# Layer 0's weight remainders: from subtractions on GpSimd to an accumulating DMA that GpSimd issues

## The chip, the cores and the metric

The kernel runs on one core of a Trainium2 chip. The metric is the device time of one execution in microseconds (us), lower is better; a kernel's time is the median of its runs. The engines are called as in the profile: PE is TensorE (PEld its weight loads), DVE is VectorE, ACT is ScalarE, POOL is GpSimd, SP is SyncE.

## The reference

One inference step of a two-layer trunk on 640 tokens of width 1024: a prompt of 128 and a latent grid of 512 (8 rows of 64). Layer 0 is a Conformer convolution branch, layer 1 a bidirectional Mamba-2 branch. The change lies in layer 0's first projection:

```python
def conformer_branch(h, on_grid, w_in, b_in, w_dw, b_dw, ln_g, ln_b, w_out):
    u = h @ w_in + b_in                       # 1024 -> 6144
    a, a_gate, z = jnp.split(u, 3, axis=-1)   # 2048 each
    v = a * jax.nn.sigmoid(a_gate)
    ...
    v = depthwise_conv(v, w_dw, b_dw).reshape(nb, length, e)   # 31 taps
    v = jax.nn.silu(layer_norm(v, ln_g, ln_b))
    return (v * jax.nn.silu(z)) @ w_out
```

All of it is float32. Before a layer come RMSNorm and a shift and scale computed from the condition (adaLN); after it comes a gated residual add.

## The kernel before

**Products in three parts.** TensorE multiplies `float32r` operands. To keep float32's precision each operand is split into a high part (a cast to `float32r`) and a low part (the value less its high part). A product is three matmuls into the same PSUM tile: high weight by high activation, high by low, low by high. A weight tile is 128 partitions x 1024 columns (512 KB); one holds all of `w_in` for 128 output columns. It is loaded by SP into `wf`, cast by ACT into `wh`, and the difference of `wf` and `wh` is written to `wl`. `wf` has two buffers, `wh` and `wl` three each. One output tile of layer 0 takes 48 matmuls: 8 chunks of the width, 2 halves of 320 tokens, 3 parts.

**Layer 0's stage.** The 6144 columns are 48 tiles: `a0` to `a15`, `g0` to `g15` (gates), `z0` to `z15`. Three are multiplied as the activations appear (`g0`, `a0`, `g1`). The other 29 `a` and `g` tiles and `z0` to `z6` stand in a list (`PLAN0`, line 457) and are multiplied in that order; the rest of `z` is multiplied behind it, under the layer norm (`z_more`, `in_tile`, `split_w`). A finished `g` tile goes through ACT's sigmoid (`after_g`, line 511, tile `sg`); the `a` tile is multiplied with it on DVE (`after_a`, line 527, tile `v`). `z` tiles go through ACT's silu (`after_z`, line 543). These steps free the PSUM buffers of the products, of which there are two (`mm`). Beside some `g` tiles PE multiplies blocks of adaLN weights (line 582), whose sums ACT copies out as `ada_row` (line 516) and PE turns (line 122).

**The convolution of `v`** is shared out by tap. ACT starts the sum in PSUM (line 625, `cva`); DVE adds most taps to it (line 633). The outer taps (`NPOOL`, 4 to 11 of 30 for each tile) are scaled by ACT into `tp` (line 664; three buffers) and added by POOL to `cv` (line 705), into which ACT first copies `cva` (line 640). POOL also makes the corrections where the two halves of the tokens meet (`seam`, lines 689 to 699). For tiles 14 and 15 POOL sums separately and DVE adds its sum at the end (line 653). `cv` and its square then feed the layer norm's column sums (line 190), at the end `pst`; then follow the statistics (lines 783 to 799) and the normalisation (lines 805 to 811).

**What sets the order.** Between `run = Order(PRIO0)` and `run.run()` the order of all five queues is planned at build time. Each chain of steps is a Python generator that yields steps (engine, planned duration), waits for keys (`key`), and takes and returns buffers (`get`, `put`). The planner keeps a clock for each engine, always emits the step that can start first (ties by `PRIO0`), and the emitted order is each engine's order: an engine never overtakes in its own queue. A step may name two engines (`either`); the later one must win by its bias. The chain `weights` loads the weight tiles, and starts for each a chain `split` (from line 474). There the cast is planned with 1.05 us on ACT; the subtraction with 2.41 on POOL or 1.23 on DVE, at a bias of 9.0 against DVE for all but the first tile. At its end `wf` is returned and the key `("w", m)` posted, on which `product(m)` waits; `product` returns `wh` and `wl` after its last matmul. The planner's clocks shape the order only; on the chip the engines wait on semaphores.

```python
for name, n in (("wf", 2), ("wh", 1), ("wl", 1), ("mm", 0), ("tm", 2), ("v", 4), ("cva", 2), ("cs", 32), ("tp", 3), ("pr", 1), ("eb", 3)):
    run.ring(name, n, 1.0 if name == "cs" else -9.0)
```

Of the kernel before, what the change touches and what calls it, by code (L numbers as in the profile page):

```python
# [7 lines left out]
F32 = mybir.dt.float32  # L8
F32R = mybir.dt.float32r
I32 = mybir.dt.int32  # L10
AF = mybir.ActivationFunctionType
ALU = mybir.AluOpType
# [29 lines left out]
def trunk(ctx: ExitStack, tc: tile.TileContext, a: dict):  # L42
# [5 lines left out]
    V, S, G, T = nc.vector, nc.scalar, nc.gpsimd, nc.tensor  # L48
# [186 lines left out]
    PE, ACT, VE, PO, SP, VL = range(6)  # L235

    class Order:
# [14 lines left out]
        def post(self, key, t):  # L252
            assert key not in self.keys, key
            self.keys[key] = t

        def put(self, name, t):
            self.rings[name].append(t)
# [73 lines left out]
    def op(eng, dur, fn, table=None):  # L331
        return "op", ((eng, dur, fn, table),)

    def either(*ways, bias=2.0):
        return "op", tuple((e_, d_, f_, None) for e_, d_, f_ in ways), bias
# [4 lines left out]
    def get(name):  # L340
        return "get", name
# [62 lines left out]
    with tc.tile_pool(name="l0", bufs=1) as lp:  # L404
# [29 lines left out]
        for i in range(3):  # L434
            t = lp.tile([P, 2, 30], F32, name=f"eb{i}")
# [24 lines left out]
        post, put, start = run.post, run.put, run.start  # L460
# [3 lines left out]
        tiles0 = [{"a": 0, "g": 16, "z": 32}[n[0]] + int(n[1:]) for n in plan if n[0] != "s"]  # L464
        W0 = {}

        def weights():
            for m in tiles0 + order[:2]:
                yield get("wf")
                wf = gp.tile([P, 1024], F32, tag="wf", bufs=2, name="wf")  # L470
                t = yield op(SP, 0.35, lambda: nc.sync.dma_start(out=wf, in_=a["w_in1"][m]))
                start(split(m, wf), t)

        def split(m, wf):
            yield get("wh")
            wh = gp.tile([P, 1024], F32R, tag="wh", bufs=3, name="wh")
            yield op(ACT, 1.05, lambda: S.copy(out=wh, in_=wf))  # L477
            yield get("wl")
            wl = gp.tile([P, 1024], F32R, tag="wl", bufs=3, name="wl")
            t = yield either((PO, 2.41, lambda: G.tensor_sub(out=wl, in0=wf, in1=wh.bitcast(F32))), (VL, 1.23, lambda: V.tensor_sub(out=wl, in0=wf, in1=wh.bitcast(F32))), bias=0.0 if m == tiles0[0] else 9.0)  # L480
            put("wf", t)
            W0[m] = wh, wl
            post(("w", m), t)
            if m in order[:2]:
                ahead.append((m, W0[m]))
# [271 lines left out]
        def w_next():  # L757
            w_out1(2)
            return wahead.pop(0)
# [77 lines left out]
        for pi, (m0, nm) in enumerate(((0, 2), (2, 4), (6, 2))):  # L837
# [3 lines left out]
            for kp in range(8):  # L841
                wh, wl = w_next()
# [4 lines left out]
            for j in range(nm):  # L847
                m = m0 + j
# [49 lines left out]
    if True:  # L898
# [8 lines left out]
        for i in range(2):  # L907
            t = lp.tile([P, 646], F32, name=f"up{i}")
# [19 lines left out]
        def tr(name):  # L928
            return lp.tile([P, NT], F32, tag="yhl", bufs=8, name=name)[:, 0:384]
# [4 lines left out]
        xr, rp, e, q, t, u, v, one = (tr(n) for n in ("xr", "rp", "e", "q", "t", "u", "v", "one"))  # L934
# [7 lines left out]
        post, put, start = run.post, run.put, run.start  # L942
# [14 lines left out]
        def w_load(i, src):  # L957
            cell = {}

            def load():  # L960
                cell["wf"] = gp.tile([P, 1024], F32, tag="wf", bufs=2, name="wf")
                nc.sync.dma_start(out=cell["wf"], in_=src)

            def high():
                cell["wh"] = gp.tile([P, 1024], F32R, tag="wh", bufs=3, name="wh")
                S.copy(out=cell["wh"], in_=cell["wf"])  # L966

            def low(e_):
                cell["wl"] = gp.tile([P, 1024], F32R, tag="wl", bufs=3, name="wl")
                e_.tensor_sub(out=cell["wl"], in0=cell["wf"], in1=cell["wh"].bitcast(F32))  # L970

            def split():
                yield get("wh")
                yield op(ACT, 1.05, high)
                yield get("wl")
                t = yield either((VL, 1.22, lambda: low(V)), (PO, 2.41, lambda: low(G)), bias=PRIO["low"])
                put("wf", t)
                W[i] = cell["wh"], cell["wl"]
                post(("w", i), t)

            yield get("wf")
            t = yield op(SP, 0.35, load)
            start(split(), t)
# [859 lines left out]
```

## Time and profile before

| | us |
|---|---|
| runs, median (3 runs) | 1106.04 (1104.78 to 1108.8) |
| the profiled execution, its own time | 1107.31 |
| its span, first to last instruction | 1105.5 |

The mean clock granted to PE was 0.986 of full speed. The kernel read 109.80 MB from HBM and wrote 4.92 MB.

How to read it: the page's first part gives busy time, share of the span and number of instructions for each engine; its second part cuts the span into 40 equal slices (27.6 us each) with the busy share in tenths. A row of a stage gives busy time and count of each engine in it, then the granted clock, the share of time that the 16 DMA engines were busy, and GB/s. A row of waits reads: who waited, line, for whom; total us, times, longest. A group's row gives the line, engine, operation, output and inputs with shapes, the count, then busy time and the mean in ns, then idle time before it and what ended that. A row of the timeline gives start and length in us, the engine, the instruction, and in brackets the idle time before it and what ended it. DMA issues aren't counted as busy time. An engine that is idle off the path that sets the end costs nothing. Matmuls overlap, so the length of one (0.31 us) is twice the 0.147 us between two.

### The profile page before, as it was taken

What the parts mean: (1) busy time and instruction counts of PE and PEld (TensorE: products, weight loads), DVE (VectorE), ACT (ScalarE), POOL (GpSimd) and SP (SyncE); (2) the same over time, 40 slices, a digit from 0 to 9 for tenths busy, and PEclk for the clock granted to TensorE, in tenths of its full rate; (3) what the DMA queues carried; (4) which work ended last, traced back from release to release, by engine and by line L of the source; (5) the groups of instructions that cost most, each with busy time, mean ns of one, the idle gap of its engine ahead of it and who ended that gap; (6) DMA issues with size and microseconds to landing.
All of it is one profiled execution on the core that took longest, in us unless ns stands there. A gap on an engine that the chain in (4) does not pass through costs nothing.

```text
span 1105.5 us, 19815 instructions
## 1 busy us (share of the span) xinstructions
PE 1057.0 (96%) x7896; PEld 980.5 (89%) x7896; DVE 816.4 (74%) x1156; ACT 590.5 (53%) x1021; POOL 521.1 (47%) x447
## 2 busy tenths in 40 slices
PE   6999899999988999999999999999999999999996
PEld 4899899998987999999999887899889888978896
DVE  2589989999889379513369789988765786767673
ACT  6546566656665466312267657493546473653442
POOL 1059999978999637300000065414551443244213
PEclk9999999999989999999999999999999999999997
DMA  9364244332212111523302363424342424343102
GB/s 360 155 210 134 70 142 133 117 133 66 69 58 77 57 40 37 193 68 116 124 10 100 96 155 105 109 73 125 101 106 90 115 64 109 109 121 95 39 20 95
DMA packets 79052, 116.00 MB, mean 105 GB/s; under 512 B 26096, under 2 KB 49008, under 8 KB 78960
## 3 DMA queue, kind: packets, MB, share of 16 engines
q1 hardware_dynamic: 78240, 113.92, 33.6%
q8 instruction: 62, 1.02, 0.4%
q10 hardware_dynamic: 720, 0.82, 0.2%
q14 instruction: 30, 0.25, 0.1%
HBM read 109.80 MB, written 4.92 MB: 104 GB/s over the span
## 4 chain that ended last, share of the span: by engine, by line
PE 56%; DVE 21%; POOL 9%; ACT 6%; issue 4%; DMA 3%; SPq 1%; POOLq 0%; DVEq 0%; ACTq 0%
DVE cva L633 9%; PE pz L1004 8%; PE o L1004 8%; PE xs L1004 6%; POOL cv L705 5%; PE o L1513 3%; PE po L1285 2%; PE pst L1222 2%; PE B L1004 2%; DVE cn L805 2%; DVE xs L1046 2%; PE py L1353 2%; POOL wl L480 2%; DVE wl L970 1%; PE C L1004 1%
## 5 line engine op out<-in xcount | busy, mean ns | idle before, releaser
L633 DVE SCALAR_TENSOR_TENSOR cva<-v,cst,cva 128x620 f32<-128x620 f32 (+11 forms) x359 | 276.0, 820 | 15.3 <-ACT cva L625 11.1
L705 POOL TENSOR_TENSOR cv<-cv,tp 128x490 f32<-128x490 f32 (+5 forms) x121 | 144.6, 1195 | 8.1
L664 ACT ACTIVATE tp<-v,cst 128x490 f32<-128x490 f32 (+5 forms) x121 | 85.7, 722 | 83.3 <-POOL cv L705 82.8
L966 ACT CAST wh<-wf 128x1024 fp32r<-128x1024 f32 x53 | 55.5, 1048 | 84.1 <-PE xs L1004 21.0
L480 POOL TENSOR_TENSOR wl<-wf,wh 128x1024 fp32r<-128x1024 f32 x37 | 89.0, 2406 | 11.7 <-ACT wh L477 11.7
L970 DVE TENSOR_TENSOR wl<-wf,wh 128x1024 fp32r<-128x1024 f32 x51 | 68.7, 1346 | 33.5 <-ACT wh L966 32.4
L1004 PE MATMUL o<-yhl,wh 128*128 128x320 f32 x384 | 92.2, 327 | 0.0
L1004 PE MATMUL pz<-h_hi,wh 128*128 128x384 f32 (+1 forms) x256 | 84.6, 331 | 0.5 <-ACT up L1033 0.5
L1291 POOL TENSOR_TENSOR y<-y,yo 128x512 f32<-128x512 f32 x32 | 44.6, 1393 | 80.1 <-DVE yo L1289 80.0
L78 ACT CAST wh<-wf 128x1024 fp32r<-128x1024 f32 (+1 forms) x37 | 31.9, 861 | 90.2 <-PE o__5110 L148 37.7
L1004 PE MATMUL pz<-h_hi,wl 128*128 128x384 f32 (+1 forms) x256 | 79.2, 309 | 0.0
L1004 PE MATMUL pz<-h_lo,wh 128*128 128x384 f32 (+1 forms) x256 | 79.1, 309 | 0.0
L1004 PE MATMUL xs<-h_hi,wh 128*128 128x384 f32 (+1 forms) x224 | 77.5, 346 | 0.0
L80 DVE TENSOR_TENSOR wl<-wf,wh 128x512 fp32r<-128x512 f32 (+1 forms) x25 | 26.5, 1061 | 67.1 <-ACT wh L78 67.1
L1004 PEld LDWEIGHTS o<-yhl,wh 128*128 128x128 f32 x384 | 63.9, 188 | 7.8 <-issue 7.8
L1046 DVE SCALAR_TENSOR_TENSOR xs<-up,cst,xs 128x642 f32<-128x642 f32 x64 | 68.0, 1064 | 2.2 <-ACT xs L1044 0.8
L1004 PE MATMUL xs<-h_hi,wl 128*128 128x384 f32 (+1 forms) x224 | 69.3, 309 | 0.0
L1004 PE MATMUL xs<-h_lo,wh 128*128 128x384 f32 (+1 forms) x224 | 69.2, 309 | 0.0
L1160 POOL TENSOR_TENSOR gb<-gb,cols 128x512 f32<-128x512 f32 x20 | 24.6, 1230 | 77.5 <-DMA gb<-acd 77.5
L1004 PE MATMUL o<-yhl,wl 128*128 128x320 f32 x192 | 59.4, 309 | 0.0
L1166 ACT ACTIVATE gf<-gf,cols 128x128 f32<-128x128 f32 x160 | 49.8, 390 | 16.4 <-DVE gf L1162 16.3
L909 POOL MEMSET up<- 128x2 f32 x2 | 0.2, 99 | 117.5 <-DVE h_lo L219 117.5
(764 smaller groups left out, 3475.8 us busy)
## 6 DMA issues: line engine op xcount, KB each, us to landing
wf<-w_in SPq DMA_DIRECT2D x48, 512.0 KB, 3.7
wa<-w_ada SPq DMA_DIRECT2D x64, 256.0 KB, 4.8
wf<-w_out SPq DMA_DIRECT2D x24, 512.0 KB, 3.9
wf<-w_xbc SPq DMA_DIRECT2D x24, 512.0 KB, 3.9
gf<-acd SPq DMA_DIRECT2D x40, 256.0 KB, 5.2
wa<-w_ada SPq DMA_DIRECT2D x16, 512.0 KB, 9.9
wf<-w_z SPq DMA_DIRECT2D x16, 512.0 KB, 3.8
gb<-acd SPq DMA_DIRECT2D x40, 128.0 KB, 4.5
```

Source lines behind the costliest of these rows:

```text
L78: S.copy(out=wh[:, :n], in_=wf[:, :n])
L480: t = yield either((PO, 2.41, lambda: G.tensor_sub(out=wl, in0=wf, in1=wh.bitcast(F32))), (VL, 1.23, lambda: V.tensor_sub(out=wl, in0=wf, ...
L633: t = yield op(VE, 0.24 + 0.01 * (hi - lo), lambda: V.scalar_tensor_tensor(out=rows64(accs[i], lo, hi), in0=rows64(vs[i], lo + d, hi + d), ...
L664: t = yield op(ACT, 0.72, lambda: S.activation(out=tp[:, :, 0 : hi - lo], in_=rows64(vs[i], lo + d, hi + d), func=AF.Copy, scale=w_dw(i, t ...
L705: t = yield op(PO, 1.12 if i < 14 else 1.3, lambda: G.tensor_add(out=rows64(cv[i], lo, hi), in0=rows64(cv[i], lo, hi), in1=sgs["tp", i, n] ...
L966: S.copy(out=cell["wh"], in_=cell["wf"])
L970: e_.tensor_sub(out=cell["wl"], in0=cell["wf"], in1=cell["wh"].bitcast(F32))
L1004: T.matmul(ps[:, b, at_ : at_ + t1 - t0], lhsT=w_, rhs=t_[:, t0:t1], start=k == 0 and n == 0, stop=k == nk - 1 and n == 2)
L1046: t = yield op(VL, 0.89, lambda: V.scalar_tensor_tensor(out=acc, in0=u[:, d : d + PW], scalar=c("w_c", j * 5 + d), in1=acc, op0=ALU.mult, ...
L1166: t = yield op(ACT, 0.39, lambda: S.activation(out=gv[:, h_, :], in_=gv[:, h_, :], func=AF.Exp, bias=cols1[ch][:, o8 + h_ : o8 + h_ + 1]), ...
L1291: t = yield op(PO, 1.29, lambda: G.tensor_add(out=y, in0=y, in1=yo))
L1513: T.matmul(ps, lhsT=wt, rhs=t_[:, tok], start=k == 0 and n == 0, stop=k == 3 and n == 2)
```

## The change

Both parts of the split are made without the subtraction. ACT casts `wf` to `wh` as before. Then ACT writes the negated high part into `wl`, and POOL issues a DMA that reads the same weight tile from HBM a second time and adds it onto `wl` (`accum_op=ALU.add`). `wf` is returned right after the cast. In the planner the new steps count 1.05 us on ACT, 1.1 us on POOL, and the weights are posted 4.0 us after that. There is no choice of engine any more. It applies to the 38 tiles that the chain `weights` handles: the 36 of the list and the first two behind it. The other splits (`split_w`, layer 1's `w_load`) are unchanged.

```diff
         def split(m, wf):
             yield get("wh")
             wh = gp.tile([P, 1024], F32R, tag="wh", bufs=3, name="wh")
-            yield op(ACT, 1.05, lambda: S.copy(out=wh, in_=wf))
+            t = yield op(ACT, 1.05, lambda: S.copy(out=wh, in_=wf))
+            put("wf", t)
             yield get("wl")
             wl = gp.tile([P, 1024], F32R, tag="wl", bufs=3, name="wl")
-            t = yield either((PO, 2.41, lambda: G.tensor_sub(out=wl, in0=wf, in1=wh.bitcast(F32))), (VL, 1.23, lambda: V.tensor_sub(out=wl, in0=wf, in1=wh.bitcast(F32))), bias=0.0 if m == tiles0[0] else 9.0)
-            put("wf", t)
+            yield op(ACT, 1.05, lambda: S.activation(out=wl, in_=wh.bitcast(F32), func=AF.Copy, scale=-1.0))
+            t = yield op(PO, 1.1, lambda: G.dma_start(out=wl, in_=a["w_in1"][m], accum_op=ALU.add))
+            t += 4.0
             W0[m] = wh, wl
             post(("w", m), t)
```

## The prediction

> **What bounds the kernel now.** The page first: who is busy, and where in the span.
>
> ```profile
> span 1105.5 us, 19815 instructions
> PE 1057.0 (96%) x7896; PEld 980.5 (89%) x7896; DVE 816.4 (74%) x1156; ACT 590.5 (53%) x1021; POOL 521.1 (47%) x447
> DVE  2589989999889379513369789988765786767673
> ACT  6546566656665466312267657493546473653442
> POOL 1059999978999637300000065414551443244213
> ```
>
> TensorE (PE) is busy for 96% of the span, so a change elsewhere can give back at most what PE waits. GpSimd (POOL) is full only in slices 4 to 13, about 83 to 360 us: the list order of layer 0, which the change touches. So I cut that stage out, 57.5 us (first product) to 355 us (end of the last tile that the list multiplies).
>
> ```profile
> core 0: us, PE busy (x) PEld busy (x) DVE busy (x) ACT busy (x) POOL busy (x), PEclk, DMA share, GB/s
> 57.50:355.00 297.50, 280.89 (x2297) 275.11 (x2297) 279.36 (x383) 177.30 (x276) 264.42 (x240) 0.98 0.34 111
> ```
>
> PE lacks 16.6 us here, VectorE (DVE) 18.1, POOL 33.1; ScalarE (ACT) has 120 us free. Three engines are nearly full, so I asked next what PE waited for up to 440 us, and what ACT waited for.
>
> ```profile
> PE u__3710 L499 <- ACT sg L511: 5.0, 1, 5.0
> PE u__4098 L157 <- ACT sz L543: 4.9, 1, 4.9
> PE u__1493 L582 <- ACT sz L543: 4.0, 1, 4.0
> PE u__3080 L122 <- ACT ada_row L516: 2.4, 1, 2.4
> ACT tp L664 <- POOL cv L705: 77.4, 65, 5.1
> ```
>
> Four waits, 16.3 us, are nearly all that PE lost in the stage, and each ends on ACT, an engine with 40% to spare. ACT is late because it runs in order and stands for 77.4 us before a convolution tap `tp`, until POOL has emptied one of the three `tp` buffers. The timeline of ACT ahead of two of the waits, and then the chain that ended last (start, length, what):
>
> ```profile
> 122.69 0.72 ACT L664 ACTIVATE tp<-v,cst 128x500 f32<-128x500 f32 x1 [4.51 <-POOL cv L705]
> 128.50 0.79 ACT L543 ACTIVATE sz<-u__1330,cst 128x640 f32<-128x640 f32 x1
> 314.23 0.71 ACT L664 ACTIVATE tp<-v,cst 128x500 f32<-128x500 f32 x1 [5.14 <-POOL cv L705]
> ```
>
> ```profile
> 131.28 7.72 PE u__1493 L499 x47
> ...
> 317.49 0.80 ACT sg L511
> 318.34 9.74 PE u__3710 L499 x48
> 328.08 7.04 PE u__3795 L499 x48
> ...
> 343.03 6.91 PE u__3967 L499 x47
> 349.96 1.04 ACT wh L78
> ...
> 354.15 0.80 ACT sz L543
> 355.00 8.60 PE u__4098 L157 x48
> ```
>
> The reader should see that the PSUM evacuations `sz` (128.50) and `sg` (317.49) come behind taps that stood 4.5 and 5.1 us for POOL. After a wait PE also starts slowly: 9.74 us for a tile that takes 7.04 undisturbed (2.7 more), 8.60 (1.6 more), 7.72 (0.7 more). So POOL, through ACT, costs PE 5.0 + 2.7 and 4.0 + 0.7, 12.4 us. The 2.4 of `ada_row` stands behind such taps too, but behind other ACT work as well: I count half, 1.2, which makes 13.6 us. The fourth wait is of another kind: ACT stood at 349.96 in a cast (L78) until PE had left the weight buffer. Its 4.9 + 1.6 us I leave in place.
>
> **The change, part by part.** *The subtraction leaves POOL.* The groups by line:
>
> ```profile
> L480 POOL TENSOR_TENSOR wl<-wf,wh 128x1024 fp32r<-128x1024 f32 x37 | 89.0, 2406 | 11.7 <-ACT wh L477 11.7
> L477 ACT CAST wh<-wf 128x1024 fp32r<-128x1024 f32 x36 | 37.6, 1044 | 15.5 <-PE u__856 L499 5.0 <-DMA wf<-w_in 4.3 <-PE u__3795 L499 2.2
> L471 SPq DMA_DIRECT2D wf<-w_in x38: 327/328/551, 26.5 to 334.4; - x38
> DMA to landing us min/median/max: 3.5/3.7/10.2
> ```
>
> 37 subtractions of 2.406 us go, 89.0 us of POOL; the 38th, on DVE, ran before the stage. 38 DMA issues come. The trace shows no DMA issued by POOL. SyncE takes 0.328 us for a 512 KB load (third row): the lower end. The upper end is the 2.406 us removed, since an issue handles no element. I take the middle, 1.4 us: 38 x 1.4 = 53, so POOL is relieved of 36 us (between 76.5 and -2.4), and falls from 264.4 to about 228 of 297.5 us, 77% busy. Then taps drain when they are ready and ACT is no longer held before the evacuations.
>
> The Trainium skill, "SBUF — State Buffer", section "Who interferes with whom", speaks against this: a GpSimd-issued DMA is starved of its descriptors while VectorE holds the shared port pair in a two-port mode. The convolution taps on DVE accumulate in PSUM, which that list does not name; no row here shows it. It would make the issue longer, the rival "dear issue" below.
>
> *A negating pass comes to ACT.* 38 activations of 128x1024; the nearest row is the cast of the same shape, 1.044 us: 39.7 us. ACT goes from 177.3 to 217 of 297.5 us, or less if the pass were shorter than the cast; no row lets it be a gain. In sum it fits in the 77.4 us that ACT stands for POOL. In place it doesn't always: queued behind it, in order, are taps, which POOL waits for, and evacuations, which PE waits for. One in three of the 36 tiles meeting it at 1.05 us would be 12.6 us, hidden while the other of two PSUM buffers is being filled for 7.04 us. I charge 3 us.
>
> *The low half lands later.* Two slots show the time there is. First the last list tile but one, `u__4098`: its buffer comes free when u__3795 ends (328.08 + 7.04 = 335.1) and is used from 350.0 on. Then `z1`, `u__1411`, the tightest:
>
> ```profile
> 335.01 1.05 ACT L477 CAST wh<-wf 128x1024 fp32r<-128x1024 f32 x1 [2.24 <-PE u__3795 L499]
> 340.00 2.43 POOL L480 TENSOR_TENSOR wl<-wf,wh 128x1024 fp32r<-128x1024 f32 x1
> 103.80 0.31 PE L499 MATMUL u__1236<-h_hi,wh 128*128 128x320 f32 x1
> 107.80 1.06 ACT L477 CAST wh<-wf 128x1024 fp32r<-128x1024 f32 x1
> 115.34 2.41 POOL L480 TENSOR_TENSOR wl<-wf,wh 128x1024 fp32r<-128x1024 f32 x1
> 118.10 0.31 PE L499 MATMUL u__1411<-h_hi,wh 128*128 128x320 f32 x1
> ```
>
> `u__4098` was ready at 342.4, 7.6 us early; `u__1411` at 117.75, 0.35 us early, because POOL held it for 6.5 us after its cast; the cast itself came 4 us after its buffer fell free (103.8, when the next tile's matmuls start). With the change: 2.1 us on ACT, 1.4 for the issue, then the landing. From 107.80 that leaves 118.1 - 107.8 - 3.5 = 6.8 us for landing and POOL's queue, from 335.0 on 11.5. No accumulating DMA is in the trace. Lower end of its landing: the plain load's median, 3.7 us; upper end: the slowest of 38 such loads, 10.2. I take 5.5, one and a half plain loads, nearer the plain row because the stage's DMA engines are busy for only 34% of the time; 38 x 0.5 MB more over 297 us add some 67 GB/s to 111. That is inside 6.8 with 1.3 us for the queue, and PE pays nothing.
>
> The Trainium skill, "Collectives: The Full Stack", section "The bandwidth ceiling: the fold count and why AG ≠ RS ≠ AR", says that a reduction in the DMA runs at half a copy's rate because it reads two sources, the addition itself being free. As an estimate from that page, twice the plain 3.7 us is 7.4 us, 0.6 us over the tightest slot: the sum would lose a microsecond or two.
>
> *Freed early, moved, and queued.* `wf` is returned after the cast; loads on SyncE start earlier and the block loads queued behind them aren't later. ACT waited 4.3 us for `wf` in all, so this is worth nothing on the path. On POOL the issue waits for ACT's negation, as the subtraction waited for the cast (11.7 us); taps queue behind it, and ACT for them: that is in the 3 us. The planner sorts all five queues anew with the new costs, so single waits will move.
>
> *The end of the stage must come forward too.* If PE is earlier, the last convolution tile must be.
>
> ```profile
> 368.19 0.82 DVE L653 TENSOR_TENSOR cv<-cv,cva 128x640 f32<-128x640 f32 x1 [9.60 <-POOL cv L705]
> 379.62 0.82 DVE L653 TENSOR_TENSOR cv<-cv,cva 128x640 f32<-128x640 f32 x1 [1.80 <-POOL cv L705]
> 395.50 0.83 DVE L805 TENSOR_TENSOR cn<-cv,mu 128x640 f32<-128x640 f32 x1 [5.88 <-ACT mu L799]
> ```
>
> The statistics of the layer norm start after 379.6, and DVE stood 9.6 + 1.8 us there for POOL. These 11.4 us are of the same cause, so the tail follows by about as much as PE gains.
>
> *The sum.* 13.6 of PE's losses go, 3 come on ACT: -10.6 us, which the tail's 11.4 cover. The profiled execution took 1107.3 us (1.8 of it around the span) and stands 1.3 above the median of the runs, 1106.0: 1107.3 - 10.6 = 1096.7, as a median 1095.4. A measurement of this kernel can tell about 0.5%, 5.5 us, from no change.
>
> **The rivals.** *Dear issue, or no relief* (same). If one issue costs POOL what the subtraction did, or ACT, late by its second pass, feeds POOL as late as POOL was, the waits stay: 1106 within 5. For it: DVE is busy for 94% of the stage and limits PE's pace anyhow (279.4 of 297.5 us). Against: 2.4 us were spent on 131,072 elements, and an issue touches none.
>
> *Late landing* (slower). With 10.2 us to landing a slot costs 2.0 (the mean of 4 and 0 from freed to cast) + 2.1 + 1.2 (one tap ahead on POOL: half a subtraction) + 1.4 + 10.2 = 16.9, against 350.0 - 335.1 = 14.9 between freeing and use; it decides from 8.2 us on. Midway, at 9.2, each of some 33 tiles is 1.0 late: +33, 1139. It would show as PE waits on a DMA, which the stage has none of now. Against it: 34% of DMA share, and a typical load at 3.7.
>
> *ACT becomes the bound* (slower). If each evacuation comes 1.05 us late and one in three then holds PE, that is the 12.6 us above, and nothing is gained because the taps wait for ACT as they did for POOL: 1118.6. For it: all four PE waits end on ACT. Against: 217 of 297 us.
>
> *All of it* (faster). If the planner's new order also clears the wait at L78: 12.4 + 2.4 + 6.5 = 21.3, 1085. PE's own work allows no more.
>
> **How the numbers follow.** Forecast -10.6: 0.45, its own range 1091 (12.4 + 2.4 and nothing lost) to 1100 (half of it kept). All of it: 0.05. No relief: 0.20. Late landing: 0.15. ACT bound: 0.15. Faster is 0.50, same 0.20, slower 0.30. The range 1088 to 1126 holds the forecast, no relief, ACT bound and the lower third of late landing; it leaves out "all of it" and the rest of late landing, under 0.2.
>
> **What would show it.** Right: POOL under 240 us busy in the stage with issues counted; ACT's wait for `cv` well below 77 us; u__3710's and u__1493's waits gone; the `cn` of 395.5 at about 385. Wrong in the landing: PE waits on a DMA into `wl`. Wrong in the issue: POOL's gaps of over 2 us around each DMA. Wrong in ACT: PE waits on `sg` or `sz` whose ACT was busy, not waiting. If the stage is shorter and the time isn't, the tail from 355 to 450 took it back.

## The result and the profile after

| | kernel before | changed kernel |
|---|---|---|
| median of 18 runs each, us | 1106.68 (1104.78 to 1109.84) | 1100.26 (1097.95 to 1103.74) |
| span of the profiled execution, us | 1105.5 | 1098.0 |

The changed kernel is 6.4 us faster: ratio 0.9942, 95% interval 0.9931 to 0.9952. The forecast was 10.6 us faster, so the direction came and about three fifths of the size; 1100.3 lies at the upper end of the forecast's own 1091 to 1100.

The page of the changed kernel, the engines and the queue that carries the new DMAs (packets, MB, share of the 16 DMA engines):

```profile
span 1098.0 us, 19890 instructions
PE 1055.7 (96%) x7896; PEld 979.0 (89%) x7896; DVE 817.2 (74%) x1155; ACT 625.8 (57%) x1059; POOL 467.6 (43%) x448
q0 software_dynamic: 5472, 19.93, 10.7%
```

POOL has 53 us less to do, ACT 35 more, PE nearly the same. The DMA issues of POOL are in its busy time here (33.2 us, row below), unlike those of SP. The changed stage, same columns as before:

```profile
57.50:355.00 297.50, 285.41 (x2324) 279.63 (x2324) 286.27 (x390) 217.40 (x320) 224.56 (x260) 0.98 0.73 176
```

POOL fell from 264.4 to 224.6 us (228 foreseen), ACT rose to 217.4 (217 foreseen), PE got 4.5 us more of its work into the same stretch, and the DMA engines went from 34% to 73% busy. What PE waited for up to 440 us, and ACT in the stage:

```profile
PE u__4136 L157 <- ACT sz L545: 4.3, 1, 4.3
PE u__775 L501 <- DMA wl<-w_in: 4.1, 1, 4.1
PE u__3759 L501 <- ACT sg L513: 2.4, 1, 2.4
ACT tp L666 <- POOL cv L707: 31.5, 38, 2.2
ACT cv L642 <- DVE cva L635: 16.0, 7, 4.4
```

Lines of this kernel stand two later than those of the kernel before, and tiles have new numbers: `u__4136` is the `u__4098` of before, `u__3759` the `u__3710`, `u__1513` the `u__1493`. The wait at `u__1493` (4.0) is gone, that at `u__3710` is halved (5.0 to 2.4), the one at the cast of L78 stays (4.9 to 4.3). ACT's wait for POOL fell from 77.4 to 31.5 us, and its wait for DVE's tap sums rose from 12.4 to 16.0. One wait is new: `u__775`, the second tile of the list, waits for the low half of its weights. The chain of the changed kernel shows where each piece of time went (start, length, what):

```profile
61.57 9.20 DMA wl<-w_in
70.82 8.54 PE u__775 L501 x46
79.36 7.04 PE u__863 L501 x48
...
132.51 7.23 PE u__1513 L501 x48
139.75 7.04 PE u__1607 L501 x48
...
314.76 7.31 PE u__3759 L501 x48
322.07 7.04 PE u__3849 L501 x48
...
348.37 9.90 PE u__4136 L157 x48
```

`u__775` ends at 79.36. Its counterpart of before started at 65.86 and the next tile's first matmul with a low half came at 73.3, so it ended near 73.2: the changed kernel is 6 us *late* here. From 79.36 on PE runs without a gap, and at the end of `u__1513` it is only 0.6 us late (139.75 against 139.14), because it no longer waits before that tile. So up to here the change has gained nothing. At the end of `u__3759` it is 6.0 us early (322.07 against 328.08): the `ada_row` wait fell from 2.4 to 0.8 us, the one for the sigmoid from 5.0 to 2.4. It is 5.3 early at the end of `u__4136` (348.37 + 9.90 = 358.3 against 355.00 + 8.60 = 363.6). In the tail:

```profile
388.06 0.83 DVE L807 TENSOR_TENSOR cn<-cv,mu 128x640 f32<-128x640 f32 x1 [6.02 <-ACT mu L801]
```

The normalisation starts at 388.06, 7.4 us before the 395.50 of the kernel before, and the end comes 7.5 us earlier. Ahead of it DVE now stands 13.0 us for PE's column sums and no longer for POOL.

The new operation itself: first its group, then the landing, from the view of its line:

```profile
L482 POOL DMA_DIRECT2D wl<-w_in x38 | 33.2, 873 | 53.3 <-ACT wl L481 33.7
```

```profile
DMA to landing us min/median/max: 5.3/6.6/10.3
```

An issue keeps POOL for 0.87 us, and the weights are there 6.6 us after it, 10.3 at worst (3.7 and 10.2 for SyncE's plain load before). The issues took 841 to 887 ns each in the stage, where DVE is busy for 286 of 297.5 us. The row thus shows no starving of the kind that the Trainium skill, "SBUF — State Buffer", section "Who interferes with whom", speaks of; whether these DVE instructions run in a mode that the section means, no run shows. Nor does the row tell whether some of it hides in the landing.

### The profile page after: what moved, and what is told of

Same layout as the page of the kernel before. It is cut to its first block, busy times and chain, and to the rows that moved or that the text cites. A ratio compares the mean times of both kernels' runs of the same rounds, so it can differ in the third digit from the quotient of the medians.

```text
span 1098.0 us, 19890 instructions
## 1 busy us (share of the span) xinstructions
PE 1055.7 (96%) x7896; PEld 979.0 (89%) x7896; DVE 817.2 (74%) x1155; ACT 625.8 (57%) x1059; POOL 467.6 (43%) x448
## 3 DMA queue, kind: packets, MB, share of 16 engines
q0 software_dynamic: 5472, 19.93, 10.7%
## 4 chain that ended last, share of the span: by engine, by line
PE 65%; DVE 19%; ACT 5%; POOL 4%; issue 4%; DMA 2%; SPq 0%; POOLq 0%; DVEq 0%; ACTq 0%
PE pz L1006 8%; PE o L1006 8%; DVE cva L635 7%; PE xs L1006 6%; POOL cv L707 3%; PE o L1515 3%; PE po L1287 2%; PE pst L1224 2%; PE B L1006 2%; PE py L1355 2%; DVE xs L1048 2%; DVE cn L807 2%; PE C L1006 1%; PE o__5617 L148 1%; PE o__5618 L148 1%
## 5 line engine op out<-in xcount | busy, mean ns | idle before, releaser
L635 DVE SCALAR_TENSOR_TENSOR cva<-v,cst,cva 128x540 f32<-128x540 f32 (+12 forms) x359 | 278.0, 821 | 10.2 <-ACT cva L627 5.2
L707 POOL TENSOR_TENSOR cv<-cv,tp 128x490 f32<-128x490 f32 (+5 forms) x121 | 149.7, 1237 | 8.2
L666 ACT ACTIVATE tp<-v,cst 128x490 f32<-128x490 f32 (+5 forms) x121 | 82.9, 715 | 31.6 <-POOL cv L707 31.5
L78 ACT CAST wh<-wf 128x1024 fp32r<-128x1024 f32 (+1 forms) x37 | 31.8, 860 | 96.2 <-PE o__5148 L148 38.9
L482 POOL DMA_DIRECT2D wl<-w_in x38 | 33.2, 873 | 53.3 <-ACT wl L481 33.7
L80 POOL TENSOR_TENSOR wl<-wf,wh 128x1024 fp32r<-128x1024 f32 (+1 forms) x12 | 26.4, 2203 | 64.3 <-ACT wh L78 64.3
```

Source lines behind the costliest of these rows:

```text
L80: sub.tensor_sub(out=wl[:, :n], in0=wf[:, :n], in1=wh[:, :n].bitcast(F32))
L482: t = yield op(PO, 1.1, lambda: G.dma_start(out=wl, in_=a["w_in1"][m], accum_op=ALU.add))
L635: t = yield op(VE, 0.24 + 0.01 * (hi - lo), lambda: V.scalar_tensor_tensor(out=rows64(accs[i], lo, hi), in0=rows64(vs[i], lo + d, hi + d), ...
L666: t = yield op(ACT, 0.72, lambda: S.activation(out=tp[:, :, 0 : hi - lo], in_=rows64(vs[i], lo + d, hi + d), func=AF.Copy, scale=w_dw(i, t ...
L707: t = yield op(PO, 1.12 if i < 14 else 1.3, lambda: G.tensor_add(out=rows64(cv[i], lo, hi), in0=rows64(cv[i], lo, hi), in1=sgs["tp", i, n] ...
```

## The experiments

**The theory**: POOL was relieved, through ACT's queue PE's evacuations came sooner, and the late landing at the second list tile gave part of it back. **The rivals**: the new planned order made the gain and POOL's relief did not; or ACT's extra pass took the rest of it. Each kernel below was timed against the kernel before; a ratio under 1 is faster than that. Edits are to the changed kernel unless another is named.

**One suspect at a time.** The first three list tiles by the old subtraction, so that nothing lands late:

```diff
+            early = m in tiles0[:3]
...
+            if early:
+                t = yield either((PO, 2.41, lambda: G.tensor_sub(out=wl, in0=wf, in1=wh.bitcast(F32))), (VL, 1.23, lambda: V.tensor_sub(out=wl, in0=wf, in1=wh.bitcast(F32))), bias=0.0 if m == tiles0[0] else 9.0)
+                put("wf", t)
+            else:
+                yield op(ACT, 1.05, lambda: S.activation(out=wl, in_=wh.bitcast(F32), func=AF.Copy, scale=-1.0))
+                t = yield op(PO, 1.1, lambda: G.dma_start(out=wl, in_=a["w_in1"][m], accum_op=ALU.add))
+                t += 4.0
```

> The first three tiles of the list (a1, g2, a2) get their low half by subtraction again, the other 35 by the accumulating DMA. In the changed kernel PE stood 4.1 us at g2 for its DMA and then took 13.19 instead of 7.30 us for the tile. My theory (the relief of POOL gave the gain, the first late landing gave part of it back): that wait goes and nothing takes its place, 5.9 us less than 1100.3, so 1094.4 (1093 to 1097). Rival 'VectorE sets the pace' (busy 286 of 297.5 us in the stage): PE waits elsewhere for as long, 1099 to 1101. Rival 'every landing is late': the fourth tile's DMA makes PE wait in turn, 1097 to 1100.

Measured: 1099.07 us, ratio 0.9938 (0.9925 to 0.995), only 1.2 us under the changed kernel, with intervals that overlap; the theory's number was missed and that of 'VectorE sets the pace' met. PE's longest wait in the stage, and ACT's timeline ahead of it:

```profile
PE u__3101 L122 <- ACT ada_row L524: 4.4, 1, 4.4
```

```profile
251.15 0.69 ACT L648 COPY cv<-cva 128x640 f32<-128x640 f32 x1 [2.06 <-DVE cva L641]
...
261.32 0.69 ACT L648 COPY cv<-cva 128x640 f32<-128x640 f32 x1 [2.01 <-DVE cva L641]
...
263.94 0.79 ACT L519 ACTIVATE sg<-u__3003,cst 128x640 f32<-128x640 f32 x1
264.63 0.26 ACT L524 COPY ada_row<-u__3003 128x128 f32<-128x128 f32 x1
```

The second tile's wait is gone, as it should be (the fourth waits 0.9 us for its DMA, as the rival 'every landing is late' had it, but no later one does). PE was 4.7 us ahead of the changed kernel until the 4.4 us at `u__3101`: ACT stood twice for DVE's finished tap sum, and a table load, `sg` and `ada_row` were behind it. With POOL out of the way the next engine of the convolution is late. The late landing is a loss one can see, but removing it hardly pays here, since PE only meets the next wait sooner. (The planner orders this kernel anew, so part of the difference can be its order.)

POOL filled up again, behind each DMA in the same step, with the planned order unchanged:

```diff
+            def issue():
+                G.dma_start(out=wl, in_=a["w_in1"][m], accum_op=ALU.add)
+                for _ in range(2):
+                    jk = tmp.tile([P, 176], F32, tag="jk", bufs=1, name="jk")
+                    G.tensor_sub(out=jk, in0=wh[:, 0:176].bitcast(F32), in1=wh[:, 512:688].bitcast(F32))
+            t = yield op(PO, 1.1, issue)
```

> Behind each of the 38 DMA issues GpSimd does two useless subtractions of 128x176 (about 1.05 us together, 40 us in all: what its busy time in the stage fell by, 264.4 to 224.6). The order of all queues stays that of the changed kernel but for a few 0.4 us steps. My theory (POOL's relief is the cause): ScalarE's wait before the taps goes from 31.5 us back to 60 to 80, PE waits on sg or sz come back, and the time is 1106 (1103 to 1110). Rival 'the new order did it': 1100 (1098 to 1102), since the order is the same.

Measured: 1117.5 us, ratio 1.0104 (1.009 to 1.0118), 17.2 above the changed kernel. The added work in the stage, and the waits:

```profile
L486 POOL TENSOR_TENSOR jk<-wh 128x176 f32<-128x176 f32 x72 | 51.5, 715 | 2.8
```

```profile
PE u__4288 L157 <- ACT sz L550: 5.9, 1, 5.9
...
PE u__3895 L506 <- ACT sg L518: 4.3, 1, 4.3
...
PE u__1557 L589 <- ACT sz L550: 2.8, 1, 2.8
...
ACT tp L671 <- POOL cv L712: 51.9, 47, 3.4
```

The row's 51.5 us lies partly under the issues; POOL's busy time over the whole kernel rises by 42.6 us, from 467.6 to 510.2, near the 40 meant and still under the 521.1 of the kernel before. The waits on `sg` (`u__3895`, the `u__3710` of before) and on `sz` (`u__1557`, the `u__1493`) are back; `u__4288` is the tile behind the cast of L78, whose wait had never gone (4.3). ACT's wait for POOL is 51.9, short of the 60 to 80 expected. In the traces PE, DVE, ACT and POOL go through the same sequence as in the changed kernel but for a few steps, so the order alone is not what made the gain. But the kernel became 11 us slower than the one before, with less work on POOL than that one, which the theory had not foreseen; the last experiment takes that up.

The negating pass written twice, at the same place:

```diff
-            yield op(ACT, 1.05, lambda: S.activation(out=wl, in_=wh.bitcast(F32), func=AF.Copy, scale=-1.0))
+            def negate():
+                for _ in range(2):
+                    S.activation(out=wl, in_=wh.bitcast(F32), func=AF.Copy, scale=-1.0)
+            yield op(ACT, 1.05, negate)
```

> ScalarE writes each negated tile twice, in the same place of the order: 38 x 1.06 = 40 us more on ScalarE, 217 to 257 of 297.5 us in the stage, and each DMA is issued 1.06 us later. My theory: the pass is mostly hidden, as I charged 3 us for the first one; the second costs 1 to 6 us, 1101 to 1106, part of it at g2 whose landing comes 1 us later. Rival 'ScalarE became the bound': 12 us or more, 1112 and up, with PE waits on sg and sz while ScalarE is busy.

Measured: 1112.59 us, ratio 1.0055 (1.0043 to 1.0068), 12.3 above the changed kernel. My small figure fell, the rival "ACT bound" gave the size. The stage, and POOL's own waiting, in the group of the issue:

```profile
57.50:355.00 297.50, 281.67 (x2273) 274.73 (x2272) 272.44 (x371) 245.67 (x346) 213.19 (x245) 0.97 0.70 170
```

```profile
L485 POOL DMA_DIRECT2D wl<-w_in x38 | 33.3, 876 | 71.3 <-ACT wl L483 61.8
```

At 245.7 of 297.5 us ACT is not full, and still a second pass of 40 us costs 12: POOL stands 61.8 us for ACT (33.7 with one pass), the taps come late, and DVE gets through 13.8 us less of its work in the stage.

The accumulation taken away: the DMA copies, so `wl` holds the whole weight in place of its low half.

```diff
-            t = yield op(PO, 1.1, lambda: G.dma_start(out=wl, in_=a["w_in1"][m], accum_op=ALU.add))
+            t = yield op(PO, 1.1, lambda: G.dma_start(out=wl, in_=a["w_in1"][m]))
```

> The DMA from GpSimd copies the weights instead of adding them (the low half then holds the whole weight, so the addition of the remainder is left out); all else, order included, is unchanged. It prices the accumulation. If reading the destination makes the landing long (6.6 us median, 9 at g2, against 3.8 for SyncE's plain loads): the landing falls to 4 to 5 us, the wait at g2 by 2 to 4 us, and the time to 1096 to 1098. If the way through GpSimd or the crowd of other loads makes it long: the landing stays within 1 us of 6.6, g2 waits as before, 1100 (1099 to 1101).

Measured: 1098.25 us, ratio 0.9927 (0.9913 to 0.9941), 2.0 under the changed kernel, with intervals that overlap. The landing fell to 4.8 us, as expected if reading the destination makes it long; the wait fell by 1.3 us where 2 to 4 were expected. The queue's row, the landing, and the one wait on it:

```profile
q0 software_dynamic: 5472, 19.93, 5.8%
```

```profile
DMA to landing us min/median/max: 3.7/4.8/8.5
```

```profile
PE u__775 L501 <- DMA wl<-w_in: 2.8, 1, 2.8
```

The same bytes take 5.8% of the DMA engines as a copy and 10.7% when they accumulate, 1.84 times as much. That is near the rule that the prediction weighed, of the Trainium skill, "Collectives: The Full Stack", section "The bandwidth ceiling: the fold count and why AG ≠ RS ≠ AR", that a reduction in the DMA runs at half a copy's rate; the section states it for collectives among several ranks, not for one core's transfer as here. The time to landing rose by less, 4.8 to 6.6 us, 1.4 times. The copy too is late at the second tile, by 2.8 us.

The copying kernel without the negating pass (the planner still counts it):

```diff
-            yield op(ACT, 1.05, lambda: S.activation(out=wl, in_=wh.bitcast(F32), func=AF.Copy, scale=-1.0))
+            yield op(ACT, 1.05, lambda: None)
```

> The DMA copies the weights, and ScalarE's negating pass is left out as well (the low half holds the whole weight); the planner still counts 1.05 us for it, so the order stays. Against the run with the copying DMA and the pass (1098.25) it prices the first pass, which takes 40 us of ScalarE. Theory 'ScalarE and GpSimd are one chain, each us on either costs about 0.3' (the doubled pass cost 12.3 us, the refilled GpSimd 17.2 us for 51.5): 8 to 12 us less, 1086 to 1090. My charge of 3 us in the prediction: 1095. Rival 'VectorE sets the pace' (busy 287 of 297.5): at most 3 us less, 1095 to 1098.

Measured: 1098.52 us, ratio 0.9925 (0.9913 to 0.9938): 0.3 over the same kernel with the pass. By the two intervals the first pass costs nothing within some 2 us. The theory, which had 8 to 12 us less, fell, and so did the 3 us of the prediction. Stage and waits:

```profile
57.50:355.00 297.50, 286.94 (x2337) 280.62 (x2336) 288.30 (x393) 180.74 (x282) 210.20 (x254) 0.98 0.54 175
```

```profile
PE u__1502 L584 <- ACT sz L545: 4.1, 1, 4.1
...
ACT tp L666 <- POOL cv L707: 34.9, 50, 2.7
ACT cv L642 <- DVE cva L635: 29.9, 11, 5.1
```

ACT has 36 us less to do, and stands 29.9 us for DVE where it stood 16.0, and 34.9 for POOL where it stood 31.5: much of the pass had lain in waits. Note the first row of the waits: without the pass the issue no longer waits for ACT, the second tile has its weights in time, and the `sz` wait of before (4.0, `u__1493`) is there as 4.1, with POOL at 210 us. The silu that it waits for started at 128.50 in the kernel before; in this kernel, and then in the changed one, it starts no sooner:

```profile
129.12 0.79 ACT L545 ACTIVATE sz<-u__1336,cst 128x640 f32<-128x640 f32 x1
```

```profile
130.42 0.79 ACT L545 ACTIVATE sz<-u__1345,cst 128x640 f32<-128x640 f32 x1
```

Where ACT stood 4.51 us for POOL before, it here stands 4.69 for DVE's `v` (to 117.61), and then has a cast, six taps and a table load to do ahead of the silu. So relieving POOL did not take this wait away; in the changed kernel PE came 6 us late and found the buffer free.

On top of the first experiment, every second tile of the list back to the subtraction, 19 DMAs left (17 of the list, and the two tiles behind it):

```diff
-            early = m in tiles0[:3]
+            early = m in tiles0[:3] or m in tiles0[4::2]
```

> The first three tiles and every second one behind them get their low half by subtraction on GpSimd, the other 17 by the accumulating DMA: half of the relief, half of the pass. If costs on GpSimd and on ScalarE add up linearly, half of the gain that is left: about 1102. If both grow faster than in proportion as each engine fills (one at 89% before, the other at 73% after), the mixture beats both: 1093 to 1097.

Measured: 1095.23 us, ratio 0.9897 (0.9883 to 0.991), 11.5 under the kernel before, one of the two best.

```profile
57.50:355.00 297.50, 291.55 (x2414) 285.05 (x2413) 283.17 (x389) 203.06 (x304) 249.74 (x255) 0.99 0.56 147
```

```profile
PE u__1496 L590 <- ACT sz L551: 1.8, 1, 1.8
```

No wait in the stage is over 1.8 us, though POOL is 249.7 us busy. Over the whole kernel POOL has 28 us less than before and ACT 19 more, and that serves PE better than 53 and 35. But not all of it is the load: in this order the silu that PE needs behind the list stands ahead of the cast of L78, and the wait there, 4.9 before and 4.3 in the changed kernel, is 0.8. Of the 14.6 us that PE is ahead of the kernel before at the end of that tile, 5.4 come there.

Two kernels moved taps, on top of the first experiment: ten of the 121 POOL taps to DVE, and the reverse.

```diff
-        NPOOL = (10, 7, 9, 7, 5, 9, 11, 5, 5, 6, 10, 10, 11, 8, 4, 4)
+        NPOOL = (9, 6, 8, 6, 5, 8, 10, 5, 5, 6, 9, 9, 10, 7, 4, 4)
```

```diff
-        NPOOL = (10, 7, 9, 7, 5, 9, 11, 5, 5, 6, 10, 10, 11, 8, 4, 4)
+        NPOOL = (11, 8, 10, 8, 5, 10, 12, 5, 5, 6, 11, 11, 12, 9, 4, 4)
```

> As the run with the first three tiles by subtraction (1099.07), and ten of the tiles give one of their outer taps from ScalarE and GpSimd to VectorE: ScalarE 10 x 0.72 = 7.2 and GpSimd 10 x 1.2 = 12 us less, VectorE 10 x 0.7 = 7 us more. Theory 'ScalarE and GpSimd are one chain': (7.2 + 12) x 0.3 = 5.8 less, 1093 (1092 to 1096). Rival 'VectorE sets the pace': up to 7 us more, 1102 to 1106.

> The opposite of the former: the same ten tiles give one tap more to ScalarE and GpSimd, using the time that GpSimd won; VectorE is 7 us lighter. Theory 'one chain': 5.8 us more, 1105 (1102 to 1108). Rival 'VectorE sets the pace': up to 7 us less than 1099.07, 1092 to 1096.

Measured: to DVE 1095.17 us, ratio 0.9897 (0.9883 to 0.991), 3.9 under the first experiment; to POOL 1106.16, ratio 0.9994 (0.9985 to 1.0003), 7.1 over it. A tap on POOL needs ACT to scale it first, one on DVE does not. The stage with taps on DVE:

```profile
57.50:355.00 297.50, 287.42 (x2386) 281.19 (x2385) 289.74 (x403) 211.06 (x310) 216.00 (x248) 0.99 0.71 174
```

DVE is 97% busy and the kernel is faster: fullness of DVE is not what holds it. Both times are those that the theory of one chain of ACT and POOL expected; as each kernel is also ordered anew, how much is load and how much order is not separated.

**Do the two gains add?** First both edits together:

```diff
+            early = m in tiles0[:3] or m in tiles0[4::2]
...
+        NPOOL = (9, 6, 8, 6, 5, 8, 10, 5, 5, 6, 9, 9, 10, 7, 4, 4)
```

> Every second tile by the accumulating DMA, and ten taps moved to VectorE: both of the runs that came to 1095.2 in one. Theory 'ScalarE and GpSimd are one chain that PE waits for': the two reliefs add up as long as PE still waits, 1095.2 - 3.9 = 1091 (1089 to 1093); PE's waits in the stage are down to about 6 us, so there is no more to win than that. Rival 'VectorE is next' (busy 283 + 7 of 297.5 us): no gain over either, 1094 to 1098.

Measured: 1098.75 us, ratio 0.9934 (0.9921 to 0.9947). They do not add, and 1091 was missed. PE's longest wait, and ACT's timeline there:

```profile
PE u__4097 L157 <- ACT sz L551: 8.9, 1, 8.9
```

```profile
338.46 1.04 ACT L78 CAST wh<-wf 128x1024 fp32r<-128x1024 f32 x1 [3.66 <-PE u__3980 L507]
...
346.65 0.79 ACT L551 ACTIVATE sz<-u__3894,cst 128x640 f32<-128x640 f32 x1
```

The cast of L78 has been put ahead of the silu that PE needs, and waits 3.66 us for PE's buffer; behind it a tap waits 2.93 for POOL. In the every-second kernel alone the planner had put that silu (340.84) ahead of its cast (341.54), and the wait was 0.8. The traces place the loss. At the end of the list PE is 11.5 us ahead of the kernel before, as with the taps alone (11.6; every second alone: 9.2), so up to there the second edit adds nothing to the first. At the end of the next tile it is 6.4 ahead, with the taps alone 10.3: this tile makes the 3.6 us by which the kernel is slower than that one. The cast was not moved by hand to test it.

Then a mixture with fewer DMAs, one tile in three of the list (11, and the two behind it: 13, where the expectation counts 12); the edit is to the every-second kernel:

```diff
-            early = m in tiles0[:3] or m in tiles0[4::2]
+            early = m in tiles0[:3] or m in tiles0[4::3] or m in tiles0[5::3]
```

> One tile in three by the accumulating DMA (12 of 38), the others by subtraction. If the best mixture lies in the middle between all by subtraction (1106.7) and all by DMA (1099 with the first three subtracted), with half at 1095.2: this one comes to 1097 to 1100. If what matters is only that the first tiles don't wait for a DMA: 1095, as half. If GpSimd's relief is what counts, in proportion: 17.2 us for 51.5 us, so 17 x 1.8 = 31 us relief give about 10 less than all by subtraction, 1096 to 1097.

Measured: 1105.11 us, ratio 0.9991 (0.9978 to 1.0004), off every expectation, and no faster than the kernel before. Its two longest PE waits in this stretch:

```profile
PE u__4111 L157 <- ACT sz L551: 5.3, 1, 5.3
PE u__1499 L590 <- ACT sz L551: 3.3, 1, 3.3
```

The evacuations of before are late again. In the stage POOL is as busy as in the every-second kernel (249.6 us), but only because less work got done in it: over the whole kernel it has 502.1 us to do, against 492.8. By the end of the tile behind the list PE is 13.7 us later than in the every-second kernel; 6.5 of that arise over the list and 7.1 at that one tile, where the cast of L78 again stands ahead of the silu and waits 3.66 us. So about half is the order at one place rather than the load. What else makes it is left open.

**Why was the refilled kernel slower than the one before?** The refilled kernel with copying DMAs and without the pass:

```diff
-            yield op(ACT, 1.05, lambda: S.activation(out=wl, in_=wh.bitcast(F32), func=AF.Copy, scale=-1.0))
+            yield op(ACT, 1.05, lambda: None)
...
-                G.dma_start(out=wl, in_=a["w_in1"][m], accum_op=ALU.add)
+                G.dma_start(out=wl, in_=a["w_in1"][m])
```

> GpSimd refilled as in the run that came to 1117.5, but the DMA copies and ScalarE's negating pass is left out (the low half holds the whole weight), the order as planned with the pass. It asks why the refilled kernel is 11 us above the kernel before, although GpSimd does no more there. If the pass is hidden only while GpSimd is light, and costs in full once both are loaded (one chain): about 11 less, 1104 to 1108. If the order planned for a light GpSimd is the cause, the pass being hidden as it was without the refill (0.3 us): 1114 to 1117.5.

Measured: 1106.79 us, ratio 1.0003 (0.9995 to 1.0012), the time of the kernel before. PE's longest waits from the first list tile on:

```profile
PE u__4250 L157 <- ACT sz L550: 4.9, 1, 4.9
PE u__1546 L589 <- ACT sz L550: 3.9, 1, 3.9
PE u__3861 L506 <- ACT sg L518: 3.4, 1, 3.4
PE u__3585 L506 <- ACT sz L550: 2.4, 1, 2.4
```

Three are at the places of before; the fourth is at another `z` tile, and the `ada_row` wait is 0.6. The pair of the copying kernels without the pass, POOL light and filled, is the cleanest test: nothing but POOL's subtractions differs (454.3 and 497.3 us over the whole kernel), and it costs 8.3 us. The wait for the sigmoid at `u__3710`'s counterpart goes from 1.5 to 3.4 us, ACT's wait for POOL from 34.9 to 53.3, but the `sz` wait at `u__1493`'s counterpart is 4.1 and 3.9: in this pair POOL's load doesn't set it.

Medians in us, by what POOL and ACT have to do:

| | POOL light | POOL filled again | difference |
|---|---|---|---|
| copying DMA, no pass | 1098.5 | 1106.8 | 8.3 |
| copying DMA, with pass | 1098.3 | not run | |
| accumulating DMA, with pass | 1100.3 | 1117.5 | 17.2 |

With a light POOL, pass and accumulation together cost 1.7 us, and the pass alone nothing that shows; with a full one they cost 10.7 together, and were not separated. Part of that is POOL's own: an accumulating issue with its two subtractions takes POOL some 2.1 us a tile (timeline rows of the two kernels), a copying one 1.8, so the doses differ by 38 x 0.3 = 11 us. At the 8.3 us that 38 x 1.2 = 46 us of subtractions cost without the pass, that explains 2 of the 10.7. For the rest there is an argument and no test: ACT and POOL are one chain. ACT scales a tap into one of three `tp` buffers, POOL empties it, the DMA issue stands among the taps and waits for ACT's pass, so delays of one are passed to the other unless one of them has slack. The second tile's wait for its DMA, 4.5 us in the refilled kernel and none here, may be part of it. One thing stays open in the table: the kernel of the last run has 497.3 us of POOL work, the kernel before 521.1, and both take the same time. Either the first 24 us of relief buy nothing, or the order, planned for a light POOL, costs what they bring.

## Why the prediction was right, and where its size failed

**POOL's relief through ACT's queue: right, and shown, but for fewer waits than counted.** Filling POOL up again, in an unchanged order, cost 17.2 us with the pass and 8.3 without it, and the wait on `sg` grew again. 31.5 us of ACT's wait are left of 77.4, as foreseen in kind.

**The issue: 1.4 us was charged, 0.87 measured.** That POOL still came to 224.6 us in the stage, near the 228 foreseen, is luck: the cheaper issue should have left about 208 (264.4 - 89.0 + 33.2), and POOL did some 16 us more of its other work within the window. Over the whole kernel the relief is 53.5 us.

**The waits that go: this was right at one place and wrong at another.** How far PE is ahead of the kernel before at the end of some tiles (us, from the timelines; minus is late; tiles by the numbers of before):

| | second tile, `u__762` | `u__1493` | end of list, `u__3967` | next, `u__4098` |
|---|---|---|---|---|
| changed kernel | -6.2 | -0.6 | 6.0 | 5.3 |
| copying DMA, no pass | 0.5 | -0.6 | 7.7 | 7.4 |
| the same, POOL filled again | 1.0 | -0.2 | -0.7 | -0.7 |
| first three subtracted | 0.3 | 4.5 | 6.7 | 6.8 |
| every second subtracted | 0.6 | 3.6 | 9.2 | 14.6 |

At `u__1493` 4.7 us (wait and slow start) were to be gained by POOL's relief. The wait row is gone, but not for that reason: the silu it waited for came later than before, and PE, 6.2 us late from the second tile, no longer had to wait for it. With the weights in time the wait is 4.1 with POOL light and 3.9 with POOL filled (second and third row). The step that was wrong is to put this wait down to POOL because ACT stood for POOL ahead of it: once POOL is out of the way ACT stands for DVE there, and the six taps planned ahead of the silu stay. (A full POOL together with the pass does delay the silu, to 132.65 in the first refill.) In orders planned anew (last two rows) the tile ends 3.6 to 4.5 us earlier; how much of that is the order is not separated. At `u__3710` 7.7 us were counted and about 5.0 came: 2.4 us of wait stay, because ACT there still has a cast, the new pass, three taps and a table load to do before `sg` (308.6 to 313.9 in its chain). Of the `ada_row` wait 1.6 went, where 1.2 was counted.

**"PE pays nothing" for the landing: this step failed.** I took 5.5 us; the median is 6.6. But the median isn't what cost: the tightest slot was named wrongly, as 6.8 us. I looked at `z1` in the middle of the list, where it never became late. The loss was at the second tile, where the pipeline of weights is just starting and PE follows at once. This is POOL and PE of the changed kernel there, then two stretches of 5 us:

```profile
61.57 0.86 POOL L482 DMA_DIRECT2D wl<-w_in  x1 [3.51 <-ACT wl L481]
```

```profile
70.82 0.64 PE L501 MATMUL u__775<-h_hi,wl 128*128 128x320 f32 x1 [4.08 <-DMA wl<-w_in]
```

```profile
66.00:71.00 5.00, 0.92 (x15) 0.48 (x4) 4.79 (x7) 1.68 (x2) 3.73 (x7) 0.98 1.07 264
71.00:76.00 5.00, 5.00 (x25) 5.00 (x26) 4.93 (x7) 1.12 (x3) 0.00 (x0) 0.68 1.06 277
```

The issue came at 61.57 behind cast and pass, the first low half was wanted 5 us later, at 66.6, and the landing took 9.2 us. Even the 5.5 us charged would have been half a microsecond late here. In the last two rows the DMA engines are at their full share (1.07 and 1.06): the loads of adaLN blocks crowd there. Other loads are late there too: the two weight loads of SP issued between 60 and 76 us took 13.3 us to land (median), against 3.8 over the kernel. That the crowd makes 9.2 out of 6.6 is inferred from this; the copying kernel was late there as well. PE lost 4.1 us of wait and near 1.8 in the slow start after it, its granted clock at 0.68 in the 5 us that follow. I had used the stage's mean DMA share of 34% for a place where the kernel before already stood at 72%:

```profile
66.00:71.00 5.00, 5.00 (x35) 5.00 (x36) 4.96 (x7) 2.65 (x5) 2.86 (x2) 1.00 0.72 254
```

**ACT's pass: 3 us charged, none measured** (-0.3, within some 2 us, and with the copying DMA). The reason given, that it lies in ACT's waits, was right. A second such pass cost 12.3: the 12.6 of the rival "ACT becomes the bound" came with the dose after this one.

**The L78 wait was rightly left in place** (it stands at the first tile behind the list, which ends at 350.07, not at 355), **and the tail did follow:** 2.1 us better than PE there (7.4 early against 5.3).

Against the 10.6 foreseen, on the profiled executions: `u__1493` with the second tile -5.3 (4.7 counted, -0.6 came), `u__3710` -2.7, L78 -0.7; ACT's pass +3, `ada_row` and the rest of the list +0.5, tail +2.1. That makes 7.5, as much as the span shrank. So the first two failed by 8 us, and a pass that cost nothing and a better tail gave 5 back; that the total came as near as it did is partly luck. The terms are not independent: without the late second tile, the first experiment gained only 1.2 us.

The rivals: "no relief" falls by ACT's wait for POOL, 31.5 of 77.4, and by the refills; "late landing" was right that a slot exists, wrong that it is every tile's. Of the signs that were named, those of POOL's relief came (under 240 us, ACT's wait down, `cn` at 388 for 385), and so did the one against the landing, a PE wait on a DMA into `wl`. The better versions, 1095.2 us, came from what the prediction had not asked: how the load is best shared between POOL, ACT and DVE, and in which order.

**Open:** what the every-third mixture loses along the list, why the taps and the every-second edit don't add there, and what a full POOL makes dear, the pass or the accumulation. No order was edited by hand.

## What to carry to other kernels

When an engine works in order, price relief by who stands behind it: here 5 us of PE's waits stood behind 77 us of waiting of an engine with 40% to spare. That an engine stood ahead of a late step does not yet say that the step comes earlier without it: look for who is next, as DVE was at `u__1493`, and at the work still queued ahead. A wait that vanishes may only have been met later. A pass is free only as long as it lies in its engine's waits: the first one cost nothing that shows, the second 12 us. For a transfer that takes the place of a computation, look at the first buffers of the pipeline and at the DMA share of that very place, not at the stage's mean, and expect that a wait taken out uncovers the next one.

## What the runs showed of the hardware

- An accumulating DMA of 512 KB issued by POOL shows as 0.87 us of POOL, a copying one as 0.57. The next POOL instruction starts 0.6 us behind the issue in both, but behind an accumulating one it takes about 0.3 us longer (two 128x176 subtractions: 1.5 against 1.23 us), so the full 0.87 counts.
- Its landing has a median of 6.6 us, against 4.8 for the copy by the same route and 3.7 for SyncE's plain load before, at 1.84 times the copy's share of the DMA engines. In the other kernels here the accumulating median lies between 5.4 (13 DMAs) and 7.5 (19).
- A 4.1 us wait of PE was followed by a granted clock of 0.68 over the next 5 us, and a tile 1.5 to 2 us longer than one without a wait (8.54 for 46 matmuls against 7.04 for 48).
